# Start addresses of the operands on chip: streamed operands to multiples of 256 bytes, weight buffers from 64 to 0, 128 and 256 modulo 512

## The chip, the core and the metric

The kernel runs on one core of a Trainium2 chip. A core has five engines that run beside each other and wait for each other through semaphores: TensorE (PE in the profile, its weight loads PEld), VectorE (DVE), ScalarE (ACT), GpSimd (POOL) and SyncE (SP, which only issues transfers here). They work on an on-chip memory of 128 partitions. A tile takes the same range of bytes in each partition, so a tile has one start address, counted in bytes from the beginning of a partition. The metric is the device time of one execution in microseconds (us); lower is better.

## The reference, cut to what matters

Two layers of an encoder over 256 tokens of width 1024, all in float32. Each layer is a gated feed-forward block, a mixer, and another feed-forward block; the mixer of the first layer is differential attention beside a depthwise convolution, that of the second a gated delta rule in both directions.

```python
def swiglu_ffn(h, w_in, w_out):          # w_in 1024 x 5632, w_out 2816 x 1024
    gate, up = jnp.split(h @ w_in, 2, axis=-1)
    return (jax.nn.silu(gate) * up) @ w_out

for l in range(2):
    x = x + 0.5 * swiglu_ffn(rms_norm(x, norm_w[l, 0]), ffn_w_in[l, 0], ffn_w_out[l, 0])
    h = rms_norm(x, norm_w[l, 1])
    x = x + (attn_conv_mixer(h, ...) if l == 0 else gated_deltanet_mixer(h, ...))
    x = x + 0.5 * swiglu_ffn(rms_norm(x, norm_w[l, 2]), ffn_w_in[l, 1], ffn_w_out[l, 1])
return rms_norm(x, final_norm_w)
```

## The kernel before

**One product, three matmuls.** The activations stand transposed, [feature, token], in blocks of 128 features by 256 tokens. A float32 product is made of three products in the type float32r (a float32 that TensorE takes in one pass): every weight block is split into `hi` and `lo`, every activation into a high and a low part, and three of the four products are added in one accumulator. `column` (lines 93 to 101 in the profile) does this for one tile of 128 output features:

```python
def column(g, out, ks, xh, xl, start=True, stop=True):
    for k in ks:
        hi, lo = block(g)
        nc.tensor.matmul(out, hi, xh[:, k, :], ...)   # L99
        nc.tensor.matmul(out, hi, xl[:, k, :], ...)   # L100
        nc.tensor.matmul(out, lo, xh[:, k, :], ...)   # L101
```

The second argument is the stationary operand, 128 x 128 weights, which a weight load (LDWEIGHTS) brings into the array ahead of the matmul; the third is the streamed operand, 256 columns of 4 bytes in each partition, so 1024 bytes. The profile writes `acc<-xh,hi`: the output, then the streamed and the stationary operand. There is one weight load for each matmul.

**Who streams what.** In the first product of a feed-forward block, and in the input projections of the mixers, `column` streams `xh` and `xl`, the two parts of the normed activations (tiles of 8 blocks, 1024 bytes from block to block). In the second product it streams `hh` and `hl`, the two parts of the hidden layer (22 blocks). The output projection of the first mixer streams `ch` and `cl` (lines 743 to 747), that of the second `oo` (lines 1294 to 1296). The gates of the delta rule (lines 810 to 812) stream `xh` and `xl` against weights in the tile `both`. The values and one gate are made the other way round by `rows` (lines 126 to 128): there the weights are streamed, 512 columns at a time, and `xh`, `xl` are stationary. The products inside the delta rule (line 985) are plain float32, 128 columns, in two passes each.

**The weights.** `split_next` reads 8 blocks of weights (512 KB) from DRAM into the tile `raw` with one transfer on SP's queue, casts them to `hi` on ScalarE (line 55), and subtracts to get `lo` on VectorE or, for a few, on GpSimd (line 56). The three tiles come from pools named raw, hi and lo: a set of pools that the whole program keeps (three buffers each), and in the feed-forward and attention phases a second set (three more), used by turns. So six tiles of 8 blocks are prefetched, three in the delta rule's phase. A tile of 8 blocks serves 24 matmuls. A buffer is written again when TensorE is done with it.

**Order.** The order of the instructions on each engine is that of the source, with a scheduler's changes; the convolution, the attention and the norms run beside the projections, a step at a time (`tick`).

**Addresses.** Tiles are placed one behind the other as their pools are opened. All blocks inside the tiles `xh`, `xl`, `hh`, `hl`, `ch`, `cl` are 1024 bytes apart, and weight blocks 512 bytes, so each tile's start modulo 512 is the start of all its blocks. In the built program these are, modulo 512:

| operand | stage | before | after |
|---|---|---|---|
| `xh`, `xl` (streamed) | everywhere | 384 | 0 |
| `hh`, `hl` (streamed) | feed-forward 1 | 256 | 0 |
| | feed-forward 2 and 3 | 64 | 256 |
| | feed-forward 4 | 96 | 0 |
| `ch`, `cl` (streamed) | output projection of the attention layer | 256 | 0 |
| `oo` (streamed) | output projection of the delta rule | 416 | 256 |
| `both` (stationary) | gates of the delta rule | 96 | 256 |
| `raw`, `hi`, `lo`, kept set | everywhere | 64 | 0 |
| `raw`, `hi`, `lo`, second set | feed-forward 1 to 3, attention | 64 | 128 |
| | feed-forward 4 | 64 | 256 |

## Time and profile before

| | us |
|---|---|
| median of three runs | 1267.43 |
| the three runs | 1266.06, 1267.43, 1270.07 |
| span of the profiled execution, first to last instruction | 1266.3 |
| VectorE busy in it | 800.1 |
| ScalarE busy | 631.2 |
| GpSimd busy | 376.5 |

For the profiled execution no time is listed beside its span; the span is 1.1 us under the median of the runs and within them. The stages follow each other in the span: feed-forward 1 to about 200 us, attention and convolution to 437, feed-forward 2 to 620, feed-forward 3 to 800, the delta rule to 1066, feed-forward 4 to the end.

How to read it: a matmul's row in the profile is about 280 ns long, though the next one starts 113 to 120 ns later, since matmuls are pipelined. So TensorE's busy share says little here; what counts is the distance from one matmul's start to the next, called the pace below. It comes from the starts in the timeline, or from the count of matmuls in a window: the window's length divided by the count, where two or three matmuls that had begun before the window are counted too.

### The profile page before, as it was taken

The numbers are of one execution on the slowest core, as the hardware profiler recorded it, in microseconds if no ns is written. First come the engines' busy times: TensorE is split into PE (matmuls) and PEld (weight loads), VectorE is DVE, ScalarE is ACT, GpSimd is POOL, SyncE is SP. The second block draws the span as 40 slices with busy tenths as digits, with TensorE's granted clock in tenths as the row PEclk, the third lists the DMA queues.
The fourth block names the chain that finished last, engine by engine and source line by source line (L and its number), as shares of the span: only waits on it lengthen the run. The fifth ranks groups of instructions, "written<-read, shape, count | busy, mean of one in ns | idle before, by whom it ended". The sixth has DMA issues, their size and how long they took to land.

```text
span 1266.3 us, 23706 instructions
## 1 busy us (share of the span) xinstructions
PE 1199.8 (95%) x9592; PEld 1164.4 (92%) x9592; DVE 800.1 (63%) x1250; ACT 631.2 (50%) x976; POOL 376.5 (30%) x322
## 2 busy tenths in 40 slices
PE   7999999997899999999999999999889987999997
PEld 7999999986679999999999999889869977999996
DVE  7665663999965766655565655577964555665541
ACT  6444445658876644444444444564433334444441
POOL 1111018979913311101311101147620035211101
PEclk9999999998989999999999999999889997999998
DMA  9855656454314555555565554446460025655540
GB/s 309 267 186 185 192 192 191 158 183 148 113 42 149 167 187 187 187 188 184 178 188 187 185 184 143 142 143 189 133 193 2 1 72 162 197 186 184 188 145 34
DMA packets 75325, 204.17 MB, mean 161 GB/s; under 512 B 15912, under 2 KB 26792, under 8 KB 75088
## 3 DMA queue, kind: packets, MB, share of 16 engines
q1 hardware_dynamic: 74208, 201.93, 49.7%
q8 instruction: 75, 1.23, 0.4%
q10 hardware_dynamic: 1008, 0.74, 0.2%
q14 instruction: 34, 0.28, 0.1%
HBM read 197.12 MB, written 7.62 MB: 162 GB/s over the span
## 4 chain that ended last, share of the span: by engine, by line
PE 56%; DVE 5%; DMA 2%; ACT 1%; issue 1%; POOL 0%; SPq 0%; DVEq 0%; ACTq 0%; POOLq 0%
PE acc L99 16%; PE acc L101 16%; PE acc L100 15%; PE acc L985 6%; DVE tmp L900 1%; DVE lo L56 1%; ACT hi L55 1%; DMA raw<-in_gd_out_dram 1%; DMA raw<-in_wi_dram 1%; DVE r L862 1%; PE tr L1151 1%; DVE kq L862 1%; PE tr L1006 0%; DMA raw<-in_gd_in_dram 0%; DMA lp<-gl 0%
## 5 line engine op out<-in xcount | busy, mean ns | idle before, releaser
L55 ACT CAST hi<-raw 128x1024 fp32r<-128x1024 f32 (+1 forms) x360 | 374.6, 1043 | 478.0 <-PE acc L100 296.1
L56 DVE TENSOR_TENSOR lo<-raw,hi 128x1024 fp32r<-128x1024 f32 (+1 forms) x305 | 387.2, 1272 | 248.5 <-ACT hi L55 244.4
L99 PE MATMUL acc<-xh,hi 128*128 128x256 f32 x1840 | 518.7, 283 | 7.9 <-DVE x L218 5.0
L101 PE MATMUL acc<-xh,lo 128*128 128x256 f32 x1840 | 516.5, 281 | 2.3 <-DVE lo L56 2.3
L100 PE MATMUL acc<-xl,hi 128*128 128x256 f32 x1840 | 517.4, 281 | 0.9 <-DVE xl L161 0.9
L99 PEld LDWEIGHTS acc<-xh,hi 128*128 128x128 f32 x1840 | 347.8, 189 | 11.5 <-issue 8.3
L101 PEld LDWEIGHTS acc<-xh,lo 128*128 128x128 f32 x1840 | 348.2, 189 | 3.2 <-DVE lo L56 2.9
L100 PEld LDWEIGHTS acc<-xl,hi 128*128 128x128 f32 x1840 | 347.7, 189 | 2.3 <-DVE xl L161 1.3
L101 PE MATMUL acc<-hh,lo 128*128 128x256 f32 x704 | 197.3, 280 | 0.0
L99 PE MATMUL acc<-hh,hi 128*128 128x256 f32 x704 | 197.3, 280 | 0.0
L100 PE MATMUL acc<-hl,hi 128*128 128x256 f32 x704 | 197.3, 280 | 0.0
L251 POOL TENSOR_TENSOR s<-s,bc 128x512 f32<-128x512 f32 x44 | 78.4, 1783 | 372.4 <-ACT s L250 372.4
L56 POOL TENSOR_TENSOR lo<-raw,hi 128x1024 fp32r<-128x1024 f32 x55 | 132.2, 2411 | 73.0 <-ACT hi L55 72.7
L99 PEld LDWEIGHTS acc<-hh,hi 128*128 128x128 f32 x704 | 133.7, 190 | 0.0
L101 PEld LDWEIGHTS acc<-hh,lo 128*128 128x128 f32 x704 | 133.7, 190 | 0.0
L100 PEld LDWEIGHTS acc<-hl,hi 128*128 128x128 f32 x704 | 133.7, 190 | 0.0
L176 POOL TENSOR_TENSOR sum<-sum,sq 128x256 f32<-128x256 f32 x41 | 40.3, 983 | 216.7 <-ACT sq L172 216.1
L478 POOL TENSOR_TENSOR y<-y,tp 128x256 f32<-128x256 f32 x80 | 70.7, 910 | 9.8 <-ACT tp L475 9.5
L447 DVE SCALAR_TENSOR_TENSOR cv<-uT,convw,cv 128x256 f32<-128x256 f32 x154 | 66.3, 481 | 0.6
L242 DVE TENSOR_TENSOR h<-acc,s 128x512 f32<-128x512 f32 x44 | 30.4, 691 | 27.6 <-PE acc L101 24.2
L249 DVE TENSOR_TENSOR s<-acc,bc 128x512 f32<-128x512 f32 x44 | 30.2, 691 | 23.0 <-PE acc L101 22.6
L161 DVE SCALAR_TENSOR_TENSOR xl<-x,normw,xh 128x256 fp32r<-128x256 f32 x48 | 36.5, 778 | 12.7 <-ACT xh L160 12.7
(260 smaller groups left out, 1413.1 us busy)
## 6 DMA issues: line engine op xcount, KB each, us to landing
raw<-in_wi_dram SPq DMA_DIRECT2D x172, 512.0 KB, 4.5
raw<-in_wo_dram SPq DMA_DIRECT2D x88, 512.0 KB, 4.4
raw<-in_ac_in_dram SPq DMA_DIRECT2D x40, 512.0 KB, 4.4
raw<-in_gd_in_dram SPq DMA_DIRECT2D x32, 512.0 KB, 3.9
raw<-in_ac_out_dram SPq DMA_DIRECT2D x16, 512.0 KB, 3.8
raw<-in_gd_out_dram SPq DMA_DIRECT2D x8, 512.0 KB, 5.4
raw<-in_wi_dram SPq DMA_DIRECT2D x8, 256.0 KB, 5.1
scr<-row SPq DMA_DIRECT2D x1, 2048.0 KB, 10.6
```

The lines of the kernel that those rows point to most:

```text
L55: nc.scalar.copy(hi[sl], raw[sl])
L56: eng.tensor_tensor(lo[sl], raw[sl], hi[sl].bitcast(F32), op=ALU.subtract)
L99: nc.tensor.matmul(out, hi, xh[:, k, :], start=start and k == ks[0], stop=False)
L100: nc.tensor.matmul(out, hi, xl[:, k, :], start=False, stop=False)
L101: nc.tensor.matmul(out, lo, xh[:, k, :], start=False, stop=stop and k == ks[-1])
L161: nc.vector.scalar_tensor_tensor(g.xl[:, f, :], x[:, f, :], w, g.xh[:, f, :].bitcast(F32), op0=ALU.mult, op1=ALU.subtract,)
L176: nc.gpsimd.tensor_tensor(self.sum, self.sum, sq, op=ALU.add)
L242: nc.vector.tensor_tensor(h, acc, s, op=ALU.mult)
L251: nc.gpsimd.tensor_tensor(s, s, over(st.bc), op=ALU.mult)
L447: nc.vector.scalar_tensor_tensor(y[:, ct, :] if j == CW - 1 and not n else cv[:, i, :], uT[:, ct, j : j + T], g.convw[:, ct, j : j + 1], c ...
L478: nc.gpsimd.tensor_tensor(y[:, ct, :], y[:, ct, :], tp, op=ALU.add)
L985: nc.tensor.matmul(ps[:, h, :], lhsT(h), rhs(h), start=True, stop=True)
```

## The change

It adds a helper that reserves bytes in a pool and uses them for nothing, calls it in front of the tiles named above, orders the first constants anew, and pads one scratch tile of the delta rule (`tmp`) from 15 x 15 to 16 x 16. No instruction is added or taken away. On TensorE, ScalarE and SyncE the order of the instructions and what each waits for are the same row by row; on GpSimd two fills at the start (`ones` and `mhalf`) change places; on VectorE two products into `tmp` that were written as 225 elements in a row are now 15 rows of 15. The docstrings are gone as well, which does nothing to the program.

```diff
+def skip(pool, n, name):
+    if n:
+        pool.tile([P, n // 4], F32, name=name)
...
-def ffn(g, wi, wo, st, wcol, aside=iter(())):
+def ffn(g, wi, wo, st, wcol, skipped, aside=iter(())):
...
+        skip(fp, skipped, "skip_h")
         hh = fp.tile([P, KF, T], F32R, name="hh")
         hl = fp.tile([P, KF, T], F32R, name="hl")
...
     nc.sync.dma_start(g.normw, a["norm_w"])
+    skip(g.const, 192, "skip_x")
     g.x = g.const.tile([P, KD, T], F32, name="x")
+    g.xh = g.const.tile([P, KD, T], F32R, name="xh")
+    g.xl = g.const.tile([P, KD, T], F32R, name="xl")
     g.ident = g.const.tile([P, P], F32, name="ident")
-    g.mhalf = g.const.tile([P, 16], F32, name="mhalf")
-    nc.gpsimd.memset(g.mhalf, -0.5)
     g.ones = g.const.tile([P, P], F32, name="ones")
     nc.gpsimd.memset(g.ones, 1.0)
-    g.xh = g.const.tile([P, KD, T], F32R, name="xh")
-    g.xl = g.const.tile([P, KD, T], F32R, name="xl")
+    g.mhalf = g.const.tile([P, 16], F32, name="mhalf")
+    nc.gpsimd.memset(g.mhalf, -0.5)
+    skip(ent(tc.tile_pool(name="skip", bufs=1)), 256, "skip_w")
     g.kept_weights = weight_pools(g, ctx, 3)
...
-def phase(g, es, n, **psum):
+def phase(g, es, n, skipped, **psum):
+    if skipped:
+        skip(es.enter_context(g.tc.tile_pool(name="skip", bufs=1)), skipped, "skip_w")
     g.weights = [g.kept_weights] + ([weight_pools(g, es, n)] if n else [])
...
+        skip(mp, 192, "skip_c")
         ch = mp.tile([P, 16, T], F32R, name="ch")
         cl = mp.tile([P, 16, T], F32R, name="cl")
         uT = mp.tile([P, KD, T + 2 * HC], F32, name="uT")
+        skip(mp, 64, "skip_y")
         y = mp.tile([P, KD, T], F32, name="y")
...
-        tmp = pk.tile([n, BB - 1, BB - 1], F32, tag=f"tmp{d}", name="tmp")
+        tmp = pk.tile([n, BB, BB], F32, tag=f"tmp{d}", name="tmp")
...
         tp = ent(tc.tile_pool(name="gdt", bufs=1))
+        skip(tp, 224, "skip_b")
         big = ent(tc.tile_pool(name="gbig", bufs=9))
...
-        phase(g, es, 3, acc=3, tr=2, cv=2, sc=1)
+        phase(g, es, 3, 128, acc=3, tr=2, cv=2, sc=1)
...
-                st = ffn(g, a["wi"][0], a["wo"][0], st, 1, ac_consts(g, a, c))
+                st = ffn(g, a["wi"][0], a["wo"][0], st, 1, 192, ac_consts(g, a, c))
...
-        st = ffn(g, a["wi"][1], a["wo"][1], st, 3)
-        st = ffn(g, a["wi"][2], a["wo"][2], st, 4)
+        st = ffn(g, a["wi"][1], a["wo"][1], st, 3, 128)
+        st = ffn(g, a["wi"][2], a["wo"][2], st, 4, 128)
...
-        phase(g, es, 0, acc=5, tr=3)
+        phase(g, es, 0, 0, acc=5, tr=3)
...
-        phase(g, es, 3, acc=4, tr=2)
+        phase(g, es, 3, 256, acc=4, tr=2)
...
-        st = ffn(g, a["wi"][3], a["wo"][3], st, None)
+        st = ffn(g, a["wi"][3], a["wo"][3], st, None, 224)
```

More of the change, by code (lines that the diff above doesn't have):

```diff
@@ L287, in start @@
     nc.sync.dma_start(g.normw, a["norm_w"])
+    skip(g.const, 192, "skip_x")
     g.x = g.const.tile([P, KD, T], F32, name="x")
+    g.xh = g.const.tile([P, KD, T], F32R, name="xh")
+    g.xl = g.const.tile([P, KD, T], F32R, name="xl")
     g.ident = g.const.tile([P, P], F32, name="ident")
+    g.ones = g.const.tile([P, P], F32, name="ones")
+    nc.gpsimd.memset(g.ones, 1.0)
     g.mhalf = g.const.tile([P, 16], F32, name="mhalf")
     nc.gpsimd.memset(g.mhalf, -0.5)
-    g.ones = g.const.tile([P, P], F32, name="ones")
-    nc.gpsimd.memset(g.ones, 1.0)
-    g.xh = g.const.tile([P, KD, T], F32R, name="xh")
-    g.xl = g.const.tile([P, KD, T], F32R, name="xl")
+    skip(ent(tc.tile_pool(name="skip", bufs=1)), 256, "skip_w")
     g.kept_weights = weight_pools(g, ctx, 3)
```

## The prediction, made before the changed kernel ran

> **What bounds the kernel now.** I read the page first: the span, the shares of busy time, the clock, the chain that ended last and the costliest groups.
>
> ```profile
> span 1266.3 us, 23706 instructions
> PE 1199.8 (95%) x9592; PEld 1164.4 (92%) x9592; DVE 800.1 (63%) x1250; ACT 631.2 (50%) x976; POOL 376.5 (30%) x322
> PEclk9999999998989999999999999999889997999998
> ...
> PE 56%; DVE 5%; DMA 2%; ACT 1%; issue 1%; POOL 0%; SPq 0%; DVEq 0%; ACTq 0%; POOLq 0%
> ...
> L55 ACT CAST hi<-raw 128x1024 fp32r<-128x1024 f32 (+1 forms) x360 | 374.6, 1043 | 478.0 <-PE acc L100 296.1
> L56 DVE TENSOR_TENSOR lo<-raw,hi 128x1024 fp32r<-128x1024 f32 (+1 forms) x305 | 387.2, 1272 | 248.5 <-ACT hi L55 244.4
> L99 PE MATMUL acc<-xh,hi 128*128 128x256 f32 x1840 | 518.7, 283 | 7.9 <-DVE x L218 5.0
> ...
> L99 PE MATMUL acc<-hh,hi 128*128 128x256 f32 x704 | 197.3, 280 | 0.0
> ```
>
> TensorE leads the chain with 56% of the span, VectorE follows with 5%. The rows of L100 and L101 have the same counts as that of L99, so 3 x 1840 = 5520 matmuls stream `xh` or `xl` and 3 x 704 = 2112 stream `hh` or `hl`, 528 in each of the four feed-forward blocks. The idle time ahead of them is 7.9 us in 1840 matmuls of L99 and nothing in the 704: they wait for nobody. ScalarE's cast of the weights (L55), on the other hand, was idle for 478.0 us, of which 296.1 us ended when TensorE had freed a buffer.
>
> So in the feed-forward blocks the pace of the matmuls is the time, and I asked for windows in which TensorE does nothing else. The columns are the window, its length, TensorE's busy time, the count of matmuls, the granted clock, and what the DMA engines did.
>
> ```profile
> core 0: us, PE busy (x), PEclk, DMA share, GB/s
> 28.00:60.00 32.00, 31.41 (x260) 1.00 0.84 289
> 80.00:130.00 50.00, 50.00 (x427) 1.00 0.57 185
> 140.00:195.00 55.00, 55.00 (x488) 1.00 0.60 193
> ...
> 440.00:540.00 100.00, 100.00 (x851) 1.00 0.58 190
> 555.00:605.00 50.00, 50.00 (x419) 1.00 0.55 179
> 625.00:725.00 100.00, 100.00 (x851) 1.00 0.59 189
> ...
> 1080.00:1180.00 100.00, 100.00 (x852) 1.00 0.59 189
> 1195.00:1250.00 55.00, 55.00 (x474) 1.00 0.34 110
> ```
>
> The clock is full in all of them, the instruction and its shape are the same, and yet the pace differs by stage. With two or three matmuls taken off each count: `xh` (start 384 modulo 512) 50.00/424.6 = 117.8 ns, and the same in all four blocks; `hh` of block 1 (start 256) 55.00/485.6 = 113.3 ns; `hh` of block 2 (start 64) 50.00/416.6 = 120.0 ns; `hh` of block 4 (start 96) 55.00/471.6 = 116.6 ns. The weights begin at 64 modulo 512 in every one. What differs is where the streamed operand begins, and the only stage in which it begins at a multiple of 256 has the shortest distance. The timeline (start, length, instruction) shows that these are steady distances and no mean over stalls; I quote the first and the last of six consecutive distances in blocks 1 and 2:
>
> ```profile
> 149.87 0.28 PE L101 MATMUL acc<-hh,lo 128*128 128x256 f32 x1
> ...
> 150.55 0.28 PE L101 MATMUL acc<-hh,lo 128*128 128x256 f32 x1
> ...
> 599.83 0.28 PE L99 MATMUL acc<-hh,hi 128*128 128x256 f32 x1
> ...
> 600.55 0.28 PE L99 MATMUL acc<-hh,hi 128*128 128x256 f32 x1
> ```
>
> 0.68/6 = 113.3 ns and 0.72/6 = 120.0 ns.
>
> Two places make the picture less simple. The output projection of the attention layer also streams from 256 (`ch`, `cl`) against weights at 64, and shows both distances; and the gates stream `xh` from 384, but against weights at 96 (tile `both`):
>
> ```profile
> 371.33 0.28 PE L743 MATMUL acc<-ch,hi 128*128 128x256 f32 x1
> ...
> 372.04 0.28 PE L743 MATMUL acc<-ch,hi 128*128 128x256 f32 x1
> ...
> 395.79 0.28 PE L746 MATMUL acc<-cl,hi 128*128 128x256 f32 x1
> ...
> 396.47 0.28 PE L746 MATMUL acc<-cl,hi 128*128 128x256 f32 x1
> ...
> 809.09 0.28 PE L812 MATMUL acc<-xh,both 128*128 128x256 f32 x1
> ...
> 809.79 0.28 PE L812 MATMUL acc<-xh,both 128*128 128x256 f32 x1
> ```
>
> Between the quoted rows lie six distances each time: 0.71 us or 118 ns at 371 us, 0.68 us or 113.3 ns at 396 us, 0.70 us or 116.7 ns in the gates. So the short distance is a state that a stream from 256 can be in or out of after a pause, and the weights' start has a say too: `xh` from 384 goes at 117.8 against 64 and at 116.7 against 96.
>
> On the second point the Trainium skill speaks the other way: its page "TensorE: Matmul & The Clock Gate", section "Step-by-step: what each phase is for", says that TensorE has two independent read ports, so that loading the next weights takes nothing from the running matmul. By that rule the weights' start would not matter. The gates' 116.7 ns beside 117.8 ns disagree, by 1.1 ns.
>
> **The change part by part.** *Streamed operands to multiples of 256.* All of them then have the alignment that block 1's `hh` has now. I take its 113.3 ns for every float32r matmul of 256 columns: it is the nearest row, the same instruction at such a start. The gain by steps:
> - `xh`, `xl`: 5520 x (117.8 - 113.3 = 4.5 ns) = 24.8 us.
> - `hh`, `hl` of blocks 2 and 3: 1056 x 6.7 ns = 7.1 us. Block 4: 528 x 3.3 ns = 1.7 us. Block 1: nothing.
> - `ch`, `cl`: 384 matmuls (4 of 128 blocks' three), a mixture of 113 and 118 ns now; at half of them, 0.9 us.
> - `oo`: 192 matmuls at the end of the delta rule, among waits; I take nothing. At most it is 192 x 6.7 ns = 1.3 us.
>
> Sum 34.5 us. Not all of it lies on the path. In the attention stage (260 to 380 us) and the delta rule (800 to 940 us) TensorE takes turns with VectorE and ScalarE, as two windows out of them show by their busy time, count and clock:
>
> ```profile
> 300.00:350.00 50.00, 39.72 (x201) 0.87 0.37 116
> ...
> 900.00:950.00 50.00, 43.93 (x280) 0.86 0.51 153
> ```
>
> Counted in the timeline, some 770 of the `xh` matmuls lie in these stages, 3.5 us of the gain; I take half, which leaves 33 us.
>
> *Weights to 0, 128 or 256.* No row shows a streamed start of 0 or 256 against such weights. From below, the rows bound a matmul at 111.6 ns, from above at 120.0 ns: the lower one is the pace of the float32 products, where each pass streams 128 columns, also with one weight load per pass (a row of the chain: start, length, count):
>
> ```profile
> 961.53 11.61 PE acc L985 x104
> ```
>
> 11.61/104 = 111.6 ns. Against 113.3 that would be 1.7 ns more for some 7900 matmuls, 13 us. I stay at 113.3, since it is the row of the same instruction, and keep both ends for the rivals.
>
> *Matmuls of 512 columns* (`rows`, 192 of them) stream the weights themselves, now from 64. They would gain at most what two of 256 gain, 9 ns each or 1.7 us, in stages full of waits; taken as nothing, at worst a loss of the same size.
>
> *Supply of weights.* 24 matmuls per tile take 2.83 us now and 2.72 us then. A tile costs VectorE 1.27 us and ScalarE 1.04 us (the rows of L56 and L55), and the transfers would rise from 190 to 198 GB/s; in 28 to 60 us they already run at 289. So the supply covers the quicker pace, and what is late next is still TensorE.
>
> *`tmp` padded, fills exchanged, constants moved.* The chain of L900 and L904 runs beside the projections of the delta rule, and what makes it long is a wait, not a pitch: the same product of 36 elements takes 2.00 us once and 0.20 us another time.
>
> ```profile
> 894.63 2.00 DVE L900 TENSOR_TENSOR tmp<-tt,lp 128x36 f32<-128x36 f32 x1
> 897.91 0.20 DVE L900 TENSOR_TENSOR tmp<-tt,lp 128x36 f32<-128x36 f32 x1
> ```
>
> Taken as nothing, with one such wait, 2 us, to either side. The two fills stand on GpSimd ahead of anything that reads them; nothing.
>
> From the median of the runs, which is 1.1 us over the profiled span: 1267.4 - 33 = 1234 us. If part of the waits move, 1229 to 1240.
>
> **The rivals.** *What matters is the distance between the streamed and the stationary start, not where the stream begins; then it is slower.* Both are read at once, and two rows speak for it: streams from 96 against 64 and from 384 against 96 both go at 116.6 to 116.7 ns, and their differences, 32 and 288, are the same modulo 256; and the worst distance, 120.0, belongs to equal starts (64 and 64). After the change equal starts modulo 256 become the rule: `xh` at 0 against the kept set at 0, everywhere. Priced so: 3050 matmuls of `xh` against the kept set and 530 against the second set of block 4 lose 2.2 ns each, 7.9 us; the 1940 against 128 I put in the middle between 117.8 and 120, 2.1 us; block 1's `hh` loses 5 to 7 ns on 528, 3.2 us; `ch` and block 4's `hh` lose 3.3 ns on 912, 3.0 us; blocks 2 and 3 gain 0.6 us. Together 16 us slower, 1283 us. It decides if `xh` against the kept set stands at 120 ns instead of under 117. Against it: the state at 113.3 in a stage of 528 matmuls without a break needs no such account. Chance 0.20.
>
> *Quicker still.* If the weights' start was what kept 113.3 from 111.6, the sum is 34.5 + 13 - 2 = 46 us: 1221 us. The Trainium skill's page "TensorE: Matmul & The Clock Gate", section "Back-to-back issue gap", gives 262 cycles of 2.4 GHz for 256 columns, 109 ns; by that figure the 7900 matmuls would give up another 20 us, an estimate of 1201 us. No float32r row here is that short. Chance 0.14 for this rival.
>
> *The good state is not entered.* `ch` shows that a stream from 256 can go at 118 for twenty microseconds. If that is what happens to `xh` after every pause, block 1's `hh` loses what blocks 2 and 3 gain (528 x 4.5 = 2.4 us against 1056 x 2.2 = 2.3 us), and the time is 1267 us: no change. Chance 0.10.
>
> *In part.* One set of weight buffers gives the short distance and the other does not: half of 33 us, 1250 us, with 1240 to 1259 around it. Chance 0.10.
>
> **How the numbers follow.** The forecast itself has 0.46: 1234 us, own range 1229 to 1240. Runs of this kernel lie within 0.3% (1266.06 to 1270.07), about what a measurement can tell from no change. Faster by more: forecast, quicker still, in part, 0.46 + 0.14 + 0.10 = 0.70; same 0.10; slower 0.20. The range goes from 1200, the quickest estimate, to 1270 with the unchanged time in it, and leaves out the slower rival alone.
>
> **What would show it.** Right: in the windows of the four feed-forward blocks the count for 50 us rises from 427 to about 444, `hh` and `xh` alike, with the clock at 1.00 and the DMA share slightly up; the stages of attention and delta rule hardly move. The rival of distances: `xh` paces at 120 in one set of buffers, visible as 24 matmuls and 24 matmuls by turns. In part: such turns with 113 in one of them. Quicker still: 450 and more per 50 us. It would be wrong also if new idle time stood ahead of L99 with ScalarE's or VectorE's split as what ended it: then the supply was nearer than I think.

## The result, and the profile after

The changed kernel is slower: 1273.92 us, median of nine runs (1269.55 to 1281.38), against 1267.43 us of the kernel before, median of nine (1262.03 to 1271.28). The ratio is 1.006, 95% interval 1.0034 to 1.0086. The profiled execution took 1277.08 us, with a span of 1275.3 us; the forecast was 1234 us, and the time lies above the range as well. What came is the first rival, the one of the difference between the two starts, at less than half of its price of 16 us.

The page has the same shape as before: the same instructions, the same chain, and no new wait ahead of TensorE. In section 5 below, the idle time ahead of the matmuls of `xh` is 7.7 us (7.9 before) and ScalarE still waits for buffers (490.1 us, 478.0 before), so the supply of weights is not what became late.

```profile
span 1275.3 us, 23706 instructions
PE 1210.4 (95%) x9592; PEld 1176.5 (92%) x9592; DVE 800.0 (63%) x1250; ACT 631.7 (50%) x976; POOL 376.8 (30%) x322
...
PE 57%; DVE 5%; DMA 2%; ACT 1%; issue 1%; POOL 0%; SPq 0%; DVEq 0%; ACTq 0%; POOLq 0%
...
L61 ACT CAST hi<-raw 128x1024 fp32r<-128x1024 f32 (+1 forms) x360 | 374.8, 1043 | 490.1 <-PE acc L106 303.3
...
L105 PE MATMUL acc<-xh,hi 128*128 128x256 f32 x1840 | 524.7, 286 | 7.7 <-DVE x L224 4.7
```

(L61 and L105 to L107 are L55 and L99 to L101 of before; the changed source is six lines longer there.)

TensorE in windows of the four feed-forward blocks, `xh` and `hh` by turns (window, length, busy time and count, granted clock, DMA share, GB/s):

```profile
35.00:130.00 95.00, 95.00 (x800) 1.00 0.62 206
145.00:200.00 55.00, 55.00 (x464) 1.00 0.56 184
455.00:545.00 90.00, 90.00 (x758) 1.00 0.56 185
558.00:608.00 50.00, 50.00 (x423) 1.00 0.56 181
630.00:730.00 100.00, 100.00 (x842) 1.00 0.57 185
...
1085.00:1185.00 100.00, 100.00 (x836) 1.00 0.59 187
1205.00:1260.00 55.00, 55.00 (x460) 1.00 0.31 101
```

In these windows the clock is full and TensorE is busy throughout, yet 100 us of `xh` hold 842 and 836 matmuls where they held 851 and 852, and where the forecast wanted some 885. The timeline of block 2 shows the turns that the first rival named, 24 matmuls of one pace and 24 of the other. The first two rows are 20 distances apart inside a tile of the kept set (0 against 0), the last two 20 distances inside a tile of the second set (0 against 128):

```profile
470.60 0.28 PE L105 MATMUL acc<-xh,hi 128*128 128x256 f32 x1
...
473.00 0.28 PE L107 MATMUL acc<-xh,lo 128*128 128x256 f32 x1
...
473.95 0.28 PE L106 MATMUL acc<-xl,hi 128*128 128x256 f32 x1
...
476.32 0.28 PE L105 MATMUL acc<-xh,hi 128*128 128x256 f32 x1
```

2.40/20 = 120.0 ns, and every single distance in that tile is 120; 2.37/20 = 118.5 ns, with single distances between 115 and 122 (118.3 ns on the mean over such tiles).

By stage (from the first matmul that streams a tile to the first that streams the next), the difference to the profiled execution of before in us: the first products of the four feed-forward blocks +3.9, +1.1, +1.5, +1.9; the second products +3.1, -0.4, -0.5, +1.8; the attention layer's projections -0.6, its output -4.5; the delta rule +2.6, its output -1.2. With 0.5 us before the first of them this makes up the 9.0 us between the two spans, within the rounding.

Some 2.5 of the 3.9 us in block 1 are not the pace. They came in its first 240 matmuls, most of them between 28 and 35 us of the span, here in the kernel before and then in the changed one:

```profile
28.00:35.00 7.00, 6.41 (x48) 1.00 0.98 371
```

```profile
28.00:35.00 7.00, 5.42 (x29) 0.76 0.99 373
```

The changed kernel idled 1 us more here, and its granted clock was 0.76. By the 240th matmul of block 1 it was 2.8 us behind, of which the pace (119.2 against 117.8 ns on the mean) makes 0.3. Of the sixteen traces below only one (`e8_by_turns_gated`) has a clock under 1.00 in this window.

The output of the attention layer got shorter although its matmuls did not get quicker (about 116 ns on the mean before, pauses left out, and 118 to 120 after). The first 23 us of that stage in the kernel before, then in the changed one:

```profile
336.60:360.00 23.40, 17.87 (x75) 0.71 0.26 82
```

```profile
343.50:367.00 23.50, 18.99 (x106) 0.93 0.27 84
```

The granted clock is 0.71 and 0.93. In the sixteen traces below a clock of 0.70 to 0.79 at this place goes with a stage of about its old length (-1.2 to +0.5 us, in five of them), and one of 0.85 to 0.93 with 2.7 to 4.8 us less (eleven). The starts do not order these: one program, run and profiled twice (`e7_constant_64` and `e16_constant_again`), stood at 0.93 with a stage of 79.2 us and at 0.70 with one of 82.9 us. So the 4.5 us go with the clock of the one execution, and what sets that clock is not shown.

### The profile page after: what moved, and what is told of

It reads as the page before. It is cut to its first block, busy times and chain, and to the rows that moved or that the text cites. A ratio compares the mean times of both kernels' runs of the same rounds, so it can differ in the third digit from the quotient of the medians.

```text
span 1275.3 us, 23706 instructions
## 1 busy us (share of the span) xinstructions
PE 1210.4 (95%) x9592; PEld 1176.5 (92%) x9592; DVE 800.0 (63%) x1250; ACT 631.7 (50%) x976; POOL 376.8 (30%) x322
## 4 chain that ended last, share of the span: by engine, by line
PE 57%; DVE 5%; DMA 2%; ACT 1%; issue 1%; POOL 0%; SPq 0%; DVEq 0%; ACTq 0%; POOLq 0%
PE acc L107 16%; PE acc L106 16%; PE acc L105 16%; PE acc L999 6%; DVE tmp L913 1%; DVE lo L62 1%; ACT hi L61 1%; DVE r L875 1%; DMA raw<-in_gd_out_dram 1%; DMA raw<-in_wi_dram 1%; PE tr L1165 0%; PE tr L1020 0%; DMA raw<-in_gd_in_dram 0%; POOL lo L62 0%; DMA lp<-gl 0%
## 5 line engine op out<-in xcount | busy, mean ns | idle before, releaser
L61 ACT CAST hi<-raw 128x1024 fp32r<-128x1024 f32 (+1 forms) x360 | 374.8, 1043 | 490.1 <-PE acc L106 303.3
L62 DVE TENSOR_TENSOR lo<-raw,hi 128x1024 fp32r<-128x1024 f32 (+1 forms) x305 | 386.1, 1267 | 257.9 <-ACT hi L61 257.4
L105 PE MATMUL acc<-xh,hi 128*128 128x256 f32 x1840 | 524.7, 286 | 7.7 <-DVE x L224 4.7
L107 PE MATMUL acc<-xh,lo 128*128 128x256 f32 x1840 | 522.5, 284 | 1.9 <-DVE lo L62 1.9
L106 PE MATMUL acc<-xl,hi 128*128 128x256 f32 x1840 | 522.7, 284 | 0.8 <-DVE xl L167 0.8
L105 PEld LDWEIGHTS acc<-xh,hi 128*128 128x128 f32 x1840 | 353.3, 192 | 11.6 <-issue 7.4
L107 PEld LDWEIGHTS acc<-xh,lo 128*128 128x128 f32 x1840 | 353.5, 192 | 2.8 <-DVE lo L62 2.5
L106 PEld LDWEIGHTS acc<-xl,hi 128*128 128x128 f32 x1840 | 353.7, 192 | 2.5 <-DVE xl L167 1.2
L105 PE MATMUL acc<-hh,hi 128*128 128x256 f32 x704 | 198.8, 282 | 0.0
L107 PE MATMUL acc<-hh,lo 128*128 128x256 f32 x704 | 198.8, 282 | 0.0
L107 PEld LDWEIGHTS acc<-hh,lo 128*128 128x128 f32 x704 | 134.2, 191 | 0.0
L105 PEld LDWEIGHTS acc<-hh,hi 128*128 128x128 f32 x704 | 134.1, 190 | 0.0
```

Source lines behind the costliest of these rows:

```text
L61: nc.scalar.copy(hi[sl], raw[sl])
L62: eng.tensor_tensor(lo[sl], raw[sl], hi[sl].bitcast(F32), op=ALU.subtract)
L105: nc.tensor.matmul(out, hi, xh[:, k, :], start=start and k == ks[0], stop=False)
L106: nc.tensor.matmul(out, hi, xl[:, k, :], start=False, stop=False)
L107: nc.tensor.matmul(out, lo, xh[:, k, :], start=False, stop=stop and k == ks[-1])
```

## The experiments

The work is that of the changed kernel in every run but `e14_before_again`, which is the kernel before once more; what differs is the bytes skipped ahead of tiles, so the edits are given as starts, with a line or two of the diff against the changed kernel or the kernel named (the other lines only put the rest back to the starts told; ... marks what is left out). "Difference" is the streamed start less the stationary one, modulo 256 bytes. The times of the kernel before, run beside them, were 1264.56 us (first four), 1264.01 us (next four) and 1264.53 us (third four), medians of 17 to 23 runs.

**First: streams alone, weights alone, and two maps of other starts.** Theory A: the difference sets the pace. Theory B: the streamed start alone. Theory C: the weights' start alone.

`e1_streams_only`: streams as in the changed kernel (0 and 256), all weights at 64; differences of 192 everywhere.

```diff
-    skip(ent(tc.tile_pool(name="skip", bufs=1)), 256, "skip_w")
+    skip(ent(tc.tile_pool(name="skip", bufs=1)), 320, "skip_w")
...
-        phase(g, es, 3, 128, acc=3, tr=2, cv=2, sc=1)
+        phase(g, es, 3, 0, acc=3, tr=2, cv=2, sc=1)
...
```

> All streamed operands as in the change (0 or 256 modulo 512), all weight buffers left at 64: the half of the change that the forecast's 33 us were worked out for. Theory A (what counts is the streamed start minus the weights' start, modulo 256): the difference is 192 everywhere, as in feed-forward 1's second product before, so 113.3 ns where the short state is entered and 117.8 where it is not; 1234 us if it is entered nearly everywhere, 1267 us if hardly anywhere. Theory B (the streamed start alone counts, and the changed kernel's loss comes from something else, such as an engine that became slower): the paces of the changed kernel, 118 to 120 ns, and 1274 us. Theory C (the weights' own start counts, 64 is better than 0, 128 or 256, whatever the stream does): faster than the changed kernel, about 1234 us, with 113.3 ns.

Measured 1251.51 us (1247.53 to 1260.3), ratio 0.99 (0.9869 to 0.993). So the half of the change that moves the streams, alone, makes the kernel faster.

`e2_weights_only`: weights as in the changed kernel (0, 128, 256), `xh` at 384 as before, `hh` at 0, 64, 64 and 96 modulo 256.

```diff
-    skip(g.const, 192, "skip_x")
+    skip(g.const, 64, "skip_x")
...
```

> The other half alone: streamed operands where they were before (xh, xl at 384; hh at 0 or 256, 64, 64, 96 modulo 256), weight buffers at 0, 128 and 256 as in the change. Theory A, by differences modulo 256: xh against the kept set 128, so 118.4 ns, against the second set 0, so 120.0 ns (feed-forward 1 to 3) and 128, so 118.4 ns (feed-forward 4); hh of block 1 120 and 118.4; hh of blocks 2 and 3 at 64 and 192, 113 to 118 ns; together about 10 us over the kernel before, 1277 us. Theory B (the streamed start alone): the paces of the kernel before, 117.8, 113.3, 120.0 and 116.6 ns, and 1267 us. Theory C (the weights' start alone): the paces of the changed kernel, 120 ns against weights at 0 and 256 and 118.4 against 128 whatever is streamed, 1274 us.

Measured 1269.03 us (1266.32 to 1271.89), ratio 1.0038 (1.0019 to 1.0056). In blocks 1 to 3 `xh` from 384 went at 120.0 ns against 128 and at 118.4 against 0: the equal starts modulo 256 are the slow ones again, at another place. In block 4, where the second set is at 256 and every difference is 128, it went at 120.0 after its first five tiles; theory A expected 118.4 there, a miss. In the delta rule of the same run a constant 128 went at 118.5 in the mean. By the time alone theory B (1267 us) would do better than A (1277 us); the paces rule it out, since B has `hh` of blocks 2 and 3 at 120.0 ns, and it went at 113.3 after its first tile.

`e3_streams64_weights128`: all streams at 64 modulo 256, all weights at 128; differences of 192 as in the first run, from starts that all differ from it.

```diff
-    skip(g.const, 192, "skip_x")
+    skip(g.const, 256, "skip_x")
...
-    skip(ent(tc.tile_pool(name="skip", bufs=1)), 256, "skip_w")
+    skip(ent(tc.tile_pool(name="skip", bufs=1)), 320, "skip_w")
...
```

> Streamed operands at 64 modulo 256 everywhere, weight buffers all at 128: neither start is the one that any stage has had with a short distance, but their difference is 192 modulo 256. Theory A: the same paces and time as with streams at 0 or 256 and weights at 64, within 0.3%. Theory B (a streamed start at a multiple of 256 is needed): 117.8 to 120 ns, 1267 to 1275 us. Theory C (weights at 64 are needed): 118.4 to 120 ns, about 1274 us.

Measured 1253.24 us (1246.91 to 1254.97), ratio 0.9907 (0.9879 to 0.9935), 1.7 us from the first run. The same windows in the first run and in this one (blocks 1, 1, 2, 3, 4):

```profile
35.00:125.00 90.00, 90.00 (x767) 1.00 0.62 209
142.00:192.00 50.00, 50.00 (x427) 1.00 0.55 187
450.00:540.00 90.00, 90.00 (x767) 1.00 0.55 187
630.00:730.00 100.00, 100.00 (x851) 1.00 0.54 188
1085.00:1185.00 100.00, 100.00 (x885) 1.00 0.56 194
```

```profile
35.00:125.00 90.00, 90.00 (x766) 1.00 0.60 211
142.00:192.00 50.00, 50.00 (x427) 1.00 0.53 184
450.00:540.00 90.00, 90.00 (x767) 1.00 0.54 186
630.00:730.00 100.00, 100.00 (x852) 1.00 0.54 186
1085.00:1185.00 100.00, 100.00 (x885) 1.00 0.57 195
```

Window by window the counts agree within one, with no start in common. That is theory A; B and C expected 1267 to 1275 us and about 1274 us here. But the rows show a second thing. One difference, 192, gives two paces: 767 matmuls in 90 us are 117.7 ns, 885 in 100 us are 113.3 ns. Block 4's `xh` had the short one in both runs, the other blocks the long one. That it was the same block in both is part of why the times are so close, and the fourth set shows that a block's pace can change from one execution to the next.

`e4_map`: kept weights 0, second set 64, `xh` at 224, `hh` at 32, 192, 352 and 320, for the differences not yet seen.

```diff
-    skip(g.const, 192, "skip_x")
+    skip(g.const, 416, "skip_x")
...
-        phase(g, es, 3, 128, acc=3, tr=2, cv=2, sc=1)
+        phase(g, es, 3, 64, acc=3, tr=2, cv=2, sc=1)
...
```

> A map: kept weights at 0, second set at 64, streamed operands at another start in each stage, so that every difference that is a multiple of 32 occurs modulo 256: xh at 224 (224 against the kept set, 160 against the second), hh of block 1 at 32 (32, 224), of block 2 at 192 (192, 128), of block 3 at 96 (96, 32), of block 4 at 64 (64, 0). Theory A: 120.0 ns at 0 and 96, 118.4 at 128, 117.8 at 64, 116.7 at 32, 113.3 or 117.8 at 192, all as seen at other absolute starts; 160 and 224 are new and may be shorter. Theory B: xh at 224 (no multiple of 256) 117.8 or more in both sets, and no difference between the two sets of weights in any stage. Theory C: the same pace against the kept set in all stages, 120 ns, and against the second set 113.3 to 117.8.

Measured 1266.31 us (1263.54 to 1271.28), ratio 1.002 (0.9995 to 1.0045): no change that can be told. With the traces of before and after, these runs give the pace of a float32r matmul of 256 columns for each difference (full clock, mean distance of starts, gaps over 150 ns left out; in the feed-forward stages, where nothing but TensorE is late, at least 160 matmuls for each pair):

| difference, modulo 256 | ns | seen at (stream, weights) modulo 512 |
|---|---|---|
| 0 | 120.0 | (64, 64), (0, 0), (0, 256), (256, 0), (384, 128), (320, 64) |
| 32 | 116.7 to 116.8 | (96, 64), (32, 0), (352, 64) |
| 64 | 113.3 or 117.8 | (384, 64), (320, 0) |
| 96 | 119.9 to 120.0 | (96, 0), (352, 0) |
| 128 | 118.2 to 118.4; 120.0 in one stage | (0, 128), (256, 128), (384, 0), (192, 64); 120.0 in block 4 at (384, 0) and (384, 256) |
| 160 | 118.7; 120.1 in one stage | (224, 64); 120.1 in block 2 |
| 192 | 113.3 or 117.8 | (256, 64), (0, 64), (64, 128), (320, 128); a mixture of 114.6 at (192, 0), by turns with 128 |
| 224 | 118.2 to 118.5 | (224, 0), (32, 64) |

So the difference alone does not say everything at 64, 192, 128 and 160. The weights-only run held a hint of what chooses at 64 and 192: `hh` of its blocks 2 and 3 met 64 and 192 by turns, tile by tile, and all of it after the first tile was short.

**Second: turns between 64 and 192.** `e5_by_turns`: streams at 64, kept weights at 0, second set at 128.

```diff
-    skip(g.const, 192, "skip_x")
+    skip(g.const, 256, "skip_x")
...
-    skip(ent(tc.tile_pool(name="skip", bufs=1)), 256, "skip_w")
+    skip(ent(tc.tile_pool(name="skip", bufs=1)), 192, "skip_w")
...
```

> All streams of the feed-forward blocks and the attention layer at 64 modulo 256, the kept weights at 0, the second set at 128: the difference (streamed start less stationary start, modulo 256) is 64 and 192 by turns, tile by tile. So far these two differences went at 113.3 ns or at 117.8 ns, for whole stages; in the weights-only run, where hh met 64 and 192 by turns, all of it went at 113.4 to 113.7. Theory A (the difference sets the pace, and a turn between 64 and 192 brings in the short state): 113.3 to 113.7 ns in xh and hh of all four feed-forward blocks; 4600 matmuls of xh outside the mixers' waits gain 4.3 ns (19.8 us), hh of blocks 2 and 3 gain 6.5 ns on 1056 (6.9 us), hh of block 4 3.2 ns on 528 (1.7 us), the attention layer's output some 4 us as in the last runs: some 33 us less than the kernel before, about 1232 us. Rival (the short state is drawn at a stage's start and the turn has nothing to do with it): some stages at 117.8, 1240 to 1255 us, as the two runs before with a constant difference of 64 or 192 gave. Rival (absolute starts): no statement that holds for the paces so far.

Measured 1240.49 us (1237.08 to 1242.62), ratio 0.9825 (0.9792 to 0.9857). That is 8 us over the sum of theory A and at the edge of the rival's 1240 to 1255; the windows below decide, with no stage at 117.8.

`e6_by_turns_elsewhere`: streams of the changed kernel (0 and 256), weights at 64 and 192. Against the changed kernel the weights alone have moved, by 64 bytes.

```diff
-    skip(ent(tc.tile_pool(name="skip", bufs=1)), 256, "skip_w")
+    skip(ent(tc.tile_pool(name="skip", bufs=1)), 320, "skip_w")
...
-        phase(g, es, 3, 256, acc=4, tr=2)
+        phase(g, es, 3, 128, acc=4, tr=2)
...
```

> The same turns at other absolute starts: streams as in the changed kernel (0 and 256), weights at 64 (kept) and 192 (second set), so differences 192 and 64 by turns. Theory A with the turn: the same paces, 113.3 to 113.7 ns in all feed-forward stages, and a time within 0.3% of the run at streams 64 and weights 0 and 128, about 1232 us. Rival (drawn at a stage's start): 1240 to 1255 us with stages at 117.8. Rival (absolute starts): a clear difference from the other run with turns.

Measured 1237.97 us (1234.96 to 1244.95), ratio 0.9811 (0.9771 to 0.9851): the same within 0.3%. Against the changed kernel's 1273.92 us that is 36 us for 64 bytes. (The two were not run on one occasion; against the kernel before beside each, the ratios are 1.006 and 0.981.)

`e7_constant_64`: the first of these with the second set at 0 as well, so a constant difference of 64.

```diff
-        phase(g, es, 3, 128, acc=3, tr=2, cv=2, sc=1)
+        phase(g, es, 3, 0, acc=3, tr=2, cv=2, sc=1)
...
```

> Streams at 64 modulo 256, all weights at 0 modulo 256: the run with turns, with the second set moved by 128, so that the difference is 64 everywhere. Theory A with the turn: without turns xh stays in the long state of the kernel before, 117.8 ns in most stages (113.3 in some), so 1248 to 1265 us, 15 to 30 us more than the run with turns. Rival (drawn at a stage's start, turns mean nothing): the same time as the run with turns, within 0.5%.

Measured 1262.45 us (1256.23 to 1266.78), ratio 0.9985 (0.996 to 1.001): without the turns the gain is gone. Windows of the four blocks, `xh` and `hh` by turns, first with the turns at streams 64, then with the constant difference:

```profile
40.00:130.00 90.00, 90.00 (x797) 1.00 0.61 216
140.00:190.00 50.00, 50.00 (x443) 1.00 0.57 196
440.00:530.00 90.00, 90.00 (x797) 1.00 0.55 196
540.00:590.00 50.00, 50.00 (x443) 1.00 0.55 189
620.00:710.00 90.00, 90.00 (x797) 1.00 0.56 195
...
1060.00:1160.00 100.00, 100.00 (x883) 1.00 0.56 194
```

```profile
35.00:130.00 95.00, 95.00 (x809) 1.00 0.61 211
142.00:192.00 50.00, 50.00 (x427) 1.00 0.54 189
445.00:540.00 95.00, 95.00 (x841) 1.00 0.56 194
547.00:597.00 50.00, 50.00 (x444) 1.00 0.54 189
625.00:725.00 100.00, 100.00 (x852) 1.00 0.55 188
...
1080.00:1180.00 100.00, 100.00 (x851) 1.00 0.54 188
```

With turns every block goes at 90/794.6 = 113.3 ns once its first tiles are past. With the constant difference only block 2 does (95/838.6 and 50/441.6, 113.3 ns); the others go at 117.8 ns.

`e8_by_turns_gated`: the first with turns, and each kept buffer padded by 128 bytes, so that the delta rule's stage, which has only the kept set, meets both differences too.

```diff
+    pad = 32 if pools is g.kept_weights else 0
...
-        p.tile([P, n, P], t, tag="w", name=m) for p, t, m in zip(pools, (F32, F32R, F32R), WEIGHTS)
+        p.tile([P, n * P + pad], t, tag="w", name=m)[:, 0 : n * P].rearrange("p (n e) -> p n e", e=P)
+        for p, t, m in zip(pools, (F32, F32R, F32R), WEIGHTS)
...
```

> The run with turns, with each kept buffer padded by 128 bytes, so that the kept set alternates in itself: raw, hi and lo's three buffers begin at 0, 128 and 256, and the delta rule's stage, which has no second set, meets differences of 64 and 192 by turns too (gates and output as well). Theory A with the turn: the feed-forward blocks as in the run with turns; the delta rule's projections 113.4 instead of 117.8 ns, at most 770 matmuls of it on the path, so 0 to 4 us less than the run with turns, about 1230 us. In the feed-forward blocks the order of the buffers is now partly two of one difference in a row; if the state needs a turn at every tile, paces between 113.3 and 117.8 show there. Rival (drawn at a stage's start): no difference by this, 1240 to 1255 us.

Measured 1236.49 us (1235.78 to 1237.78), ratio 0.9797 (0.9766 to 0.9828), the fastest of all, though its interval overlaps those of the other two with turns. The delta rule's projections were 3.5 us shorter than in the first run with turns (206.7 and 210.2 us), but that does not show the turns at work there: their distance was 117.1 ns on the mean, not the 113.4 expected, and with constant differences of 64 or 192 the same stage took 206.8 to 212.0 us in other runs.

**Third: which turns, how many, and the worst case.** From the traces with turns I had formed a theory, that a turn from 64 to 192 brings the short pace in and one from 192 to 64 does not.

`e9_one_turn_up`: all weights at 0, `xh` at 64, `hh` at 192 modulo 256, so one such turn in each block. `e10_one_turn_down`: the roles exchanged. Diffs against the kernel with the constant difference:

```diff
-                st = ffn(g, a["wi"][0], a["wo"][0], st, 1, 384, ac_consts(g, a, c))
+                st = ffn(g, a["wi"][0], a["wo"][0], st, 1, 0, ac_consts(g, a, c))
...
```

```diff
-    skip(g.const, 256, "skip_x")
+    skip(g.const, 384, "skip_x")
...
-    skip(ent(tc.tile_pool(name="skip", bufs=1)), 192, "skip_w")
+    skip(ent(tc.tile_pool(name="skip", bufs=1)), 64, "skip_w")
...
```

> All weights at 0 modulo 256, xh and xl at 64, hh and hl at 192: differences 64 in the first product of each feed-forward block and 192 in the second, so one turn from 64 to 192 in each block, without a pause. In the traces so far a turn from 64 to 192 brought the short pace (113.3 ns) in within three matmuls in 33 of 46 cases, and one from 192 to 64 in 2 of 20; once in, the short pace outlived 737 of 739 turns. Theory A with the turn up: hh of all four blocks at 113.3 ns, whatever xh went at before (59.8, 59.9, 68.4 and 71.4 us for the four stages, where 62.2, 62.2, 70.8 and 73.2 are the lengths at 117.8); xh itself at 117.8 mostly. About 12 us less than the kernel before, 1252 us, less by 4.4 us for each stage of xh that enters the short pace by itself. Rival (any change of difference does it, or a draw at the stage's start): no difference in the hh stages from the kernel with xh at 192 and hh at 64.

> The same with the roles exchanged: xh and xl at 192, hh and hl at 64, all weights at 0 modulo 256, so that the turn in each block goes from 192 to 64. Theory A with the turn up: a turn down brings nothing in, so hh keeps the pace that xh had at the end of its stage, 117.8 ns where xh was at 117.8; stages of 62.2 us (twice), 70.8 and 73.2 us, and 6 to 10 us more in all than with the turn up, 1256 to 1265 us. Rival (any change does it): hh at 113.3 in all four blocks, the same time as the other. Rival (a draw at the stage's start): hh short in some blocks and long in others, whatever xh was.

Measured 1264.41 us (1257.89 to 1270.11), ratio 0.9994 (0.9972 to 1.0017), with the turn up, and 1252.29 us (1248.82 to 1259.01), ratio 0.9905 (0.9869 to 0.9941), with the turn down. Both miss, in opposite directions, and the theory falls in this form: `hh` was at 117.8 ns in all eight stages. Even where `xh` had the short pace, the turn of the stream ended it. Block 1 with the turn up, `xh` and then `hh`:

```profile
35.00:125.00 90.00, 90.00 (x796) 1.00 0.62 218
140.00:190.00 50.00, 50.00 (x427) 1.00 0.53 186
```

In the profiled execution of the turn down the gain is that of `xh`, which was short in blocks 2 and 4.

`e11_one_buffer`: the constant difference of 64, but one of the six weight buffers moved by 128 bytes.

```diff
-    g.weights = [g.kept_weights] + ([weight_pools(g, es, n)] if n else [])
+    g.weights = [g.kept_weights]
+    if n:
+        two = weight_pools(g, es, n - 1)
+        skip(es.enter_context(g.tc.tile_pool(name="skip1", bufs=1)), 128, "skip_o")
+        one = weight_pools(g, es, 1)
+        g.weights = [g.kept_weights, two, g.kept_weights, two, g.kept_weights, one]
...
```

> The kernel with a constant difference of 64 (1262 us), with one of the six weight buffers moved by 128: the difference is 64 for five tiles of weights and 192 for the sixth. The constant-difference kernel shows mostly 117.8 ns. Theory A with the turn up: the first such tile brings the short pace in, and it stays, so nearly the same as with turns at every tile: 113.3 ns in the feed-forward stages after their first 3 to 18 us, 1236 to 1245 us. Rival (the short pace belongs to tiles in a constant rhythm of two differences): 113.3 only in the tiles next to the moved buffer, about two of six, 1254 to 1260 us. Rival (draw at the stage's start): as with the constant difference, 1256 to 1267 us.

Measured 1242.28 us (1235.75 to 1244.38), ratio 0.9802 (0.9767 to 0.9837), as with turns at every tile. The timeline shows the entry in block 1: eight distances ahead of the moved buffer, whose first matmul starts at 50.99 us, eight in it, and eight in the next, which is at the old start again:

```profile
49.93 0.28 PE L105 MATMUL acc<-xh,hi 128*128 128x256 f32 x1
...
50.87 0.28 PE L107 MATMUL acc<-xh,lo 128*128 128x256 f32 x1
...
51.55 0.28 PE L107 MATMUL acc<-xh,lo 128*128 128x256 f32 x1
...
52.46 0.28 PE L106 MATMUL acc<-xl,hi 128*128 128x256 f32 x1
...
53.71 0.28 PE L105 MATMUL acc<-xh,hi 128*128 128x256 f32 x1
...
54.61 0.28 PE L107 MATMUL acc<-xh,lo 128*128 128x256 f32 x1
```

0.94/8 = 117.5 ns, 0.91/8 = 113.8 ns and 0.90/8 = 112.5 ns, by rows rounded to 10 ns; over 24 matmuls 117.7, 113.4 and 113.3 ns. One moved buffer brings the short pace in, and it stays for the five tiles that lie at the old start. In the four kernels with such buffers I counted the boundaries between two tiles that no pause of over 150 ns comes near (six distances ahead, nine behind). A turn of the weights from 64 to 192 changed a long pace into the short one in 30 of 46 cases, one from 192 to 64 in 3 of 21, a boundary without a turn in none of 61; and a short pace outlived all 787 turns.

`e12_all_equal`: every start at 0 modulo 256, against the kernel with the constant difference.

```diff
-    skip(g.const, 256, "skip_x")
+    skip(g.const, 192, "skip_x")
...
-    skip(ent(tc.tile_pool(name="skip", bufs=1)), 192, "skip_w")
+    skip(ent(tc.tile_pool(name="skip", bufs=1)), 256, "skip_w")
...
```

> All streams and all weights at 0 modulo 256, the gates' and the output's tiles too: the difference is 0 everywhere. Theory A: 120.0 ns in every feed-forward stage, without two states; against the kernel before 2.2 ns on 4224 matmuls of xh (9.3 us), 6.7 ns on 528 of hh in block 1 (3.5), 3.3 ns on 528 in block 4 (1.7), nothing in blocks 2 and 3, about 2 us in the delta rule, 3 to 4 less in the attention layer's output as in the changed kernel: about 12 us more, 1276 us (1271 to 1283). Rival (streams that begin at multiples of 256 are quick, and the changed kernel is held up by its second set of weights at 128 and 256): less than the changed kernel's 1274 us by 5 us or more.

Measured 1280.11 us (1276.52 to 1285.39), ratio 1.0124 (1.009 to 1.0157). Streams that all begin at multiples of 256 give the slowest kernel of all, with one pace in all feed-forward stages once their first tiles are past, here in blocks 1 and 2 (`xh`, `hh`, `xh`, `hh`):

```profile
35.00:130.00 95.00, 95.00 (x794) 1.00 0.60 206
145.00:200.00 55.00, 55.00 (x461) 1.00 0.55 182
450.00:550.00 100.00, 100.00 (x835) 1.00 0.54 185
560.00:610.00 50.00, 50.00 (x419) 1.00 0.52 179
```

100/832.6 and 50/416.6 are 120.1 and 120.0 ns.

**Fourth: fixed or drawn.** The forecast's row, block 1's `hh` at 113.3 ns, was still without a cause. `e13_start_mod_512` repeats block 1's starts modulo 512 relative to the weights (320, then 192); the other three are kernels run once more for a second profile, with no edit.

```diff
-    skip(g.const, 256, "skip_x")
+    skip(g.const, 0, "skip_x")
...
-    skip(ent(tc.tile_pool(name="skip", bufs=1)), 192, "skip_w")
+    skip(ent(tc.tile_pool(name="skip", bufs=1)), 448, "skip_w")
...
```

> All weights at 0 modulo 512, xh and xl at 320, hh and hl at 192 in blocks 1, 3 and 4 and at 448 in block 2. Differences modulo 256 as in the kernel with xh at 64 and hh at 192, where hh went at 117.8 in all four blocks. Modulo 512 the stream's turn is from 320 to 192 in blocks 1, 3 and 4, as in block 1 of the kernel before (384 and 256 against 64), and not in block 2. Theory M (the turn counts modulo 512): hh at 113.3 in blocks 1, 3, 4 and at 117.8 in block 2. Theory W (the short pace comes in with a change of the weights' start, and a change of the stream's start leaves the long one; block 1 of the kernel before was a draw): 117.8 in all four, or short in a block or two without that pattern.

> The kernel before, once more, for a second profile: is the pace of a stage fixed by the program or drawn in each execution? Drawn: at least one of the twelve stages changes between 113.3 and 117.8 (block 1's hh, or xh in a block). Fixed: hh of block 1 at 113.3 and xh at 117.8 in all four blocks, as in the first profile.

> The kernel with xh at 64 and hh at 192 once more: in its first profile xh of block 1 went at 113.3 and the other seven feed-forward stages at 117.8. Drawn: another pattern. Fixed: the same one.

> The kernel with a constant difference of 64 once more: in its first profile both stages of block 2 went at 113.3 and the other six feed-forward stages at 117.8. Drawn: another pattern, with hh and xh of one block alike again (nothing there turns between them). Fixed: the same one.

Measured, one run each: 1262.77, 1261.88, 1259.6 and 1262.34 us, with the kernel before at 1261.61 us beside them. `hh` went at 117.8 in all four blocks, with 320 and then 192 (blocks 1, 3 and 4) as with 320 and then 448 (block 2), so the starts modulo 512 do not fix the short pace of block 1. The kernel before, block 1's `xh` and `hh`, first in the execution on which the prediction was made and then in the second one:

```profile
35.00:130.00 95.00, 95.00 (x809) 1.00 0.64 208
142.00:192.00 50.00, 50.00 (x443) 1.00 0.60 194
```

```profile
35.00:125.00 90.00, 90.00 (x796) 1.00 0.62 217
142.00:192.00 50.00, 50.00 (x427) 1.00 0.55 189
```

The paces have changed places: `hh` 50/440.6 = 113.5 ns and then 50/424.6 = 117.8 ns, `xh` 95/806.6 = 117.8 ns and then 90/793.6 = 113.4 ns. The same program, and another draw. The constant difference of 64 drew block 1 short instead of block 2, and the turn up drew `hh` of blocks 2 and 4 short, which had been long. Over all profiles with a constant difference of 64 or 192 inside a stage, `xh` was short in 8 of 40 feed-forward stages. `hh` kept the pace of `xh` in 16 of 16 where the difference stayed the same from one to the other; where the stream turned it by 128, it was short in 3 of 18, and never in the 4 that followed a short `xh`.

## Why the prediction was wrong, step by step

*The step that failed* is the first of the change's parts: "I take its 113.3 ns for every float32r matmul of 256 columns: it is the nearest row, the same instruction at such a start." It took one stage for a rule on the streamed start. The runs show two errors in it. The start of the stream alone sets nothing: from 0 and 256 matmuls went at 120.0, 118.3, 117.8 and 113.3 ns, by the weights they met and by the draw. And the row itself was drawn: the kernel before gave 117.8 ns for it in its second profile.

The prediction's own fences had what would have spoken against the step. The gates' 116.7 ns and block 4's 116.6 ns fit a difference of 32, and the worst pace stood at equal starts; that became a rival with 0.20 when it accounted for every pace, except that 64 and 192 needed the two paces which `ch` showed. The argument against it, "the state at 113.3 in a stage of 528 matmuls without a break needs no such account", is the same reading of a single draw.

*The first rival's terms.* Its mechanism was right, its size not: 16 us were priced, 6.5 us came by the medians and 9.0 us by the profiled spans. `xh` against the kept set did stand at 120.0 ns. The 118.9 ns taken for 128, midway, was 118.3. `xh` was priced at 7.9 and 2.1, so 10.0 us, in the blocks and the mixers together. In the four blocks its stages rose by 8.4 us, of which some 5.9 are left for the pace when the 2.5 us of block 1's start are taken off; the attention layer's projections fell by 0.6 and the delta rule's rose by 2.6. Block 1's `hh` was priced at 3.2 us, and rose by 3.1, though from a draw that could have been otherwise; blocks 2 and 3 at -0.6, and fell by 0.9. The term that missed is `ch`, priced with block 4's `hh` at 3.0 us: block 4 rose by 1.8, but the stage of `ch` fell by 4.5 with a higher granted clock, which no term had.

*The weights' start.* The prediction kept 111.6 and 120.0 ns as bounds and stayed at 113.3; the upper bound was the answer for more than half of them. The Trainium skill's page "TensorE: Matmul & The Clock Gate", section "Step-by-step: what each phase is for", gives TensorE two independent read ports, so that loading the next weights takes nothing from the running matmul. The constant difference and the turns disagree: with the streams and the kept set in place and the second set moved by 128 bytes, `xh` of block 1 goes at 117.8 or at 113.3 ns. For these float32r matmuls the pace is not independent of where the weights lie.

*The good state is not entered* had 0.10, and was right about `xh` and 64 or 192, where the long pace is what four of five stages draw. It was not this kernel's case, since the change left no difference of 64 or 192 in a feed-forward block. *In part* did not come; half of the buffers differed from the other half, but by 1.7 ns, and both were slower than `xh` before.

*Supply, `tmp`, fills, clock.* Costed at nothing. For the supply that held: the idle time ahead of L105 is 7.7 us against 7.9. Of `tmp` and the fills nothing can be told: the delta rule's projections rose by 2.6 us, and in the other kernels with the padded `tmp` they took 206.7 to 212.0 us, on both sides of the 208.0 before. The clock was not nothing: in the profiled execution a lower one, with the idle time beside it, cost some 2.5 us in block 1, and a higher one went with 4.5 us less in the stage of `ch`.

*What is open.* The table gives the pace for each difference, and no run shows why, nor why 128 went at 120.0 in one stage and at 118.2 to 118.5 in the others, or 160 at 120.1 and at 118.7. Nor is it shown why a turn of the weights' start brings the short pace in while one of the stream's start ends it, or why mostly from 64 to 192. What draws the pace of a stage with one constant difference is open too.

## What to carry to other kernels

Where TensorE streams and loads weights back to back, list for each stage the streamed start less the stationary start modulo 256 beside the measured distance of matmuls, and move one of the two by 64 or 128 bytes before anything larger is tried: here equal starts cost 1280 us and turns between 64 and 192 cost 1237, with the same instructions. Alignment to a round number is worth nothing by itself, and is the worst choice if both operands get it. A row that carries a forecast should be read in two executions first.

## What the runs showed of the hardware

- The distance of float32r matmuls of 256 columns, one weight load each, clock 1.00, depends on the difference of the two starts modulo 256: 120.0 ns at 0 and 96, 116.7 at 32, 118.2 to 118.5 at 224, 118.7 or 120.1 at 160, 118.2 to 118.5 or 120.0 at 128, and 113.3 or 117.8 at 64 and 192.
- At a constant 64 or 192 a feed-forward stage of 500 to 1000 matmuls keeps the pace that it has entered within its first tiles; 8 of 40 stages of `xh` kept the short one, and one program gave another pattern in another execution. A single buffer of weights at 128 bytes' distance in a round of six is enough to bring the short one in (1242 us against 1262 us).
- The Trainium skill's page "TensorE: Matmul & The Clock Gate", section "Back-to-back issue gap", lists 262 cycles for 256 columns as the distance of isolated matmuls, an estimate of 109 ns at the 2.4 GHz it names. No feed-forward stage of any run came under 113.3 ns.
